# The FFN gate's modulation vector computed by ScalarE and GpSimd during the scans instead of by TensorE within w_in

## The chip, the cores and the metric

The kernel runs on one core of one Trainium2 chip. The metric is the device time of one execution in microseconds (us); lower is better. The core's engines are TensorE (PE in the profile, its weight loads PEld), VectorE (DVE), ScalarE (ACT), GpSimd (POOL) and SyncE (SP), which here only issues DMAs. Each engine works through its own queue in order and waits on semaphores for the others.

## The reference

One layer over 512 latent tokens and 128 context tokens, 640 rows (T) of width 2048 (D). Both groups share the weights; each has its own conditioning vector and so its own modulation:

```python
mod_ctx = (jax.nn.silu(c_ctx) @ w_mod[l] + b_mod[l])
mod_lat = (jax.nn.silu(c) @ w_mod[l] + b_mod[l])
sh1, sc1, g1, sh2, sc2, g2 = jnp.split(mod, 6, axis=-1)      # six vectors of 2048
h = rmsnorm(x, norm1_g) * (1.0 + sc1) + sh1
p = h @ w_in                                                 # 2048 x 5408
o_a, s_fin = rwkv7_bidir(shift(p[..., :3360]), s0)           # scans over the tokens, both ways, 16 heads of 64
o_b = chunk_gmlp(gelu(p[..., 3360:]))
x = x + g1 * (concat([o_a, o_b]) @ w_out)
h = rmsnorm(x, norm2_g) * (1.0 + sc2) + sh2
ff = (silu(h @ w_ffn_gate) * (h @ w_ffn_up)) @ w_ffn_down
x = x + g2 * ff                                              # g2 is used nowhere else
```

The change is about `g2`, the FFN gate: a product of two vectors (latent and context) with the last 2048 of the 12288 columns of `w_mod`, 16.8 MB of float32, plus a bias.

## The kernel before

The stages follow one another in time (us from the start of the profiled execution): the first modulation groups and the norm (to about 120), the w_in projection with everything that prepares the scans (to about 1076), the scans with half of w_out (to about 1382), the rest of w_out with the second norm (to about 1503), and the FFN (to the end).

- **Products in two parts.** Weights arrive as float32 (`raw`). ScalarE rounds them (`hi`, L173), VectorE takes the rest (`lo`, L174), and TensorE multiplies each with the activations in three matmuls of 320 columns. `split` does this for 512 x 128 weights; its tiles come from a pool of three (`st`).
- **w_in.** A loop runs over 160 pieces (40 column blocks of 128, four pieces each; three blocks come earlier). After each piece, `MODR` more steps of the generator `mod_all` are taken. `mod_all` computes four modulation groups one after the other, in the order 2, 4, 3, 5; group 5 is `g2`. Its matmuls (L913, `pm<-wt,cT`) have a weight of two columns (the two conditioning vectors) and 512 moving columns, four of them side by side in the array; then come four transposes (L181) and copies into `modc[g]`.
- **Scans.** Eight head pairs, 13 hops apart, are scanned in 117 hops. A hop advances the active pairs (`recur`): state products on TensorE (`w_ps` L1158, `u_ps` L1178, `s_ps` L1205, `y_ps` L1131 and L1141); `u_ps` is copied into the record `rec` by VectorE (L1182) and ScalarE (L1183), and `s_ps` needs both copies. ScalarE copies the outputs into `Y` (L1146). The records come by DMA (`rec<-d_S`, L1092), eight in flight, each load waiting until an older record has been used. After a pair, `norm` runs on GpSimd (L1240, L1242, L142, L1249, L1252) with squares on ScalarE (L1246) and sums on VectorE (L1247). Every hop also does a share of the w_out products (L1046 to L1048), whose weights go through `split`.
- **Order.** TensorE's order in w_in is the kernel's own by pace rules and by hand; in the scans it is the program's order. The other engines' queues, SP's too, are put in order by a scheduler when the kernel is built: an instruction that is added can move others.
- **w_out, second part.** For each of two halves of the rows and 16 blocks m, `four_blocks` does products (L1489 to L1491), and the tiles `xo1_j`, `xo2_j` (pool `xep`) are first written in its second half.

Of the kernel before, what the change touches and what calls it, by code (L numbers as in the profile page):

```python
# [10 lines left out]
F32 = mybir.dt.float32  # L11
F32R = mybir.dt.float32r
BF16 = mybir.dt.bfloat16
AF = mybir.ActivationFunctionType
ALU = mybir.AluOpType
# [4 lines left out]
P = 128  # L20
D = 2048
KB = D // P
T = 640
NT = T // P
HALF = T // 2
# [21 lines left out]
WAIT = 20  # L47
NW = 8
SUBST = 4.6
MODR = 1.36  # L50
NREC = 8
CHK = (3, 3, 4, 4, 4, 4)
POOLK = (3,)
# [36 lines left out]
def flow_step(ctx: ExitStack, tc, x_prompt, x_sample, state_rwkv, c, c_ctx, w_mod, b_mod,  # L90
# [3 lines left out]
    nc = tc.nc  # L94
    V, S, G, TE = nc.vector, nc.scalar, nc.gpsimd, nc.tensor
# [13 lines left out]
    def tpool(**a):  # L109
        if a.get("space") != DRAM:  # L110
            a["reuse_waits"] = "tile"
        return tc.tile_pool(**a)
# [35 lines left out]
    modc = {g: cp.tile([P, KB, 2], F32, name=f"modc{g}") for g in (2, 3, 4, 5)}  # L148
    cT = cb.tile([P, 2 * KB + 32], F32, name="cT")
# [63 lines left out]
    with ExitStack() as ph:  # L213
# [133 lines left out]
        for j in range(4):  # L347
# [5 lines left out]
            for kb in range(4 * j, 4 * j + 4):  # L353
                hf = p0b.tile([P, T], F32, name="hf")
# [547 lines left out]
        return quad  # L902

    def mod_all():
        for g in (2, 4, 3, 5):
            pm = cur["psum"].tile([P, 512], F32, tag="pmod", name=f"pm{g}")
            quad = load_mod(g, 0)
            for _ in range(4):
                yield
            for kb in range(0, KB, 2):  # L910
                for u in range(2):
                    for j in range(4):
                        TE.matmul(pm[32 * j:32 * j + 2, :], cT[:, 2 * (kb + u):2 * (kb + u) + 2], quad[:, u, j, :],  # L913
                                  start=(kb + u == 0), stop=(kb + u == KB - 1), tile_position=(0, 32 * j))
                for _ in range(2):
                    yield
                if kb + 2 < KB:
                    quad = load_mod(g, kb + 2)
                    for _ in range(4):
                        yield  # L920
            ms = cur["pool"].tile([P, 2, 4, 512], F32, tag=cur["raw"], name=f"ms{g}", bufs=1)[:, 0, 0, :]
            G.memset(ms, 0.0)
            for j in range(4):
                for v in range(2):
                    nc.sync.dma_start(ms[32 * j + v:32 * j + v + 1, :],
                                      b_mod[:, g * D + 512 * j:g * D + 512 * j + 512])
            yield
            yield
            for j in range(4):
                V.tensor_add(ms[32 * j:32 * j + 2, :], pm[32 * j:32 * j + 2, :], ms[32 * j:32 * j + 2, :])  # L930
            mod_cols(cur["tp"], ms, modc[g], tag=cur["tag"])
            yield
# [6 lines left out]
    g = 0  # L939
# [81 lines left out]
    xep = xex.enter_context(tpool(name="xep", bufs=1, side="right"))  # L1021
    obp = [obx.enter_context(tpool(name=n, bufs=1, side="right")) for n in ("oba", "obb")]
    pbig = obx.enter_context(tpool(name="pbig", bufs=2, space=PSUM))
    o_hi, o_lo = {}, {}

    def o_load(kb, src=None):

# [34 lines left out]
    with ExitStack() as ph:  # L1062
# [221 lines left out]
        def wout_b():  # L1284

            for q in range(2):
# [3 lines left out]
                for m in range(KB):  # L1290
# [6 lines left out]
                    for k, c in enumerate(wout(m, q)):  # L1297
                        yield c
                        if q == 0 and k in (0, 2):
# [3 lines left out]
                                TE.transpose(ps[:, t - t0, :], xc[:, t, :], ident)  # L1303
                            S.copy(xc[:, t0:t1, :], ps[:, 0:t1 - t0, :])

        for _ in range(4):
            load_next()
        load_s0(0)
# [15 lines left out]
        with tc.manual_schedule(engines={mybir.EngineType.PE}):  # L1324
            for hop in range(hops):
                if hop == OFF * nxt and nxt < NPAIR:
                    act.append((nxt, recur(nxt)))
                    nxt += 1
                for p, gen in act:
                    next(gen)  # L1330
                for job in list(after):
                    if job[0] < 0:
                        next(job[2], None)
                    elif job[0] in (LATE, LATE + 1):
                        join(job[1], job[0] - LATE)
                for p, gen in list(act):
                    if next(gen, 0) == 0:
                        act.remove((p, gen))
                        after.append([-7, p, norm(p)])
                for job in list(after):  # L1340
                    if job[0] in (LATE + 2, LATE + 3):
                        gate(job[1], job[0] - LATE - 2)
                    job[0] += 1
                    if job[0] > LATE + 3:
                        after.remove(job)
                m3.run(max(0.0, m3.left - REST * 3.2) / (hops - hop))
                if hop == hops - 12:
                    for kb in range(4):
                        o_load(kb)

            assert not act
            (_, p, gen), = after
            for _ in gen:
                pass
            for i, work in enumerate((lambda: join(p, 0), lambda: join(p, 1), lambda: gate(p, 0), lambda: gate(p, 1))):
                while m3.left > (4 - i) * 1.6 - 0.1:
                    m3.run(0.01)
                work()
            m3.drain()
        for kb in range(4, 7):  # L1360
            o_load(kb)
        o_load(7, U[7].bv)
# [74 lines left out]
    with ExitStack() as ph:  # L1437
# [40 lines left out]
        def four_blocks(hf, m, q):  # L1478

            s = slice(HALF * hf, HALF * hf + HALF)  # L1480
            if q == 0:
                pool = pb2 if m % 2 or hf == 0 and m == 4 else pbig
                banks[m] = pool.tile([P, HALF], F32, tag="big", name="big")
            ps = banks[m]
            hi, lo = split(w_out[0, 4 * q * P:(4 * q + 4) * P, m * P:(m + 1) * P], 4,
                           *((wraw, wo) if q or hf or m >= AHEAD else ()))
            for k in range(4):
                kb = 4 * q + k
                TE.matmul(ps, hi[:, k, :], o_hi[kb][:, s], start=(kb == 0), stop=False)  # L1489
                TE.matmul(ps, hi[:, k, :], o_lo[kb][:, s], start=False, stop=False)  # L1490
                TE.matmul(ps, lo[:, k, :], o_hi[kb][:, s], start=False, stop=(kb == 7))  # L1491
            return ps

        for m in range(AHEAD):
            four_blocks(0, m, 0)
        for hf in range(2):
            s = slice(HALF * hf, HALF * hf + HALF)
            for m in range(KB):
                if hf or m >= AHEAD:
                    four_blocks(hf, m, 0)  # L1500
                ps = four_blocks(hf, m, 1)
                if hf and m in (6, 7, 8, KB - 1):
                    for _ in range(2):
                        next(first)
                if sqs and (sqs[0][0] and sqs[0][1] >= 12 or m % 4 == 1):
                    stats()
                add_out(m, [ps, ps], hf)
                nc.sync.dma_start(d_x1[m][:, s], x1T[m][:, s])
                squares(hf, m)
                if hf and m > 1:  # L1510
                    for kb in HALVES[m - 2:m - 1] if m < 14 else HALVES[2 * m - 16:2 * m - 14]:
                        first_half(kb)
                    if 4 <= m < 12:
                        j, i = divmod(m - 4, 2)
                        operand(1 + i, j, x1T[j + 8 * i][:, t1])
# [620 lines left out]
```

## Time and profile before

| what | value |
|---|---|
| median of 3 runs | 3207.54 us (3205.68 to 3216.92) |
| profiled execution | 3204.18 us, span of its instructions 3202.4 us |
| TensorE clock granted, mean | 0.992 |
| TensorE busy | 3084.3 us, 96% of the span |
| VectorE, ScalarE, GpSimd busy | 2341.2, 1461.4, 1220.5 us |
| HBM read | 437.79 MB |

A busy TensorE is not TensorE at its peak, since matmuls overlap: each of the 320-column matmuls is shown with about 310 ns but the next one starts about 147 ns later. A wait row names the engine and line that waited, and what ended the wait; idle time of an engine that nobody waits for costs nothing. Times in the stretches are from the profiled execution's start.

### The profile page before, as it was taken

How to read it: one execution, taken by the hardware profiler on the slowest of the kernel's cores; microseconds unless marked ns; L12 is line 12 of the kernel's file. 1: busy time of each engine (PE TensorE's matmuls, PEld its weight loads, DVE VectorE, ACT ScalarE, POOL GpSimd, SP SyncE). 2: the span in 40 equal slices, each digit the busy share in tenths (PEclk: the TensorE clock that was granted, in tenths of full speed). 3: DMA queues.
4: the chain of work that ended last, by engine and by line, in shares of the span. 5: the costliest groups of instructions: out<-in, count | busy, mean ns of one | idle time of the engine just before them, and what ended most of it. 6: DMA issues, size and time to landing. Idle time of an engine off the chain costs nothing.

```text
span 3202.4 us, 72234 instructions
## 1 busy us (share of the span) xinstructions
PE 3084.3 (96%) x28216; PEld 2859.1 (89%) x28216; DVE 2341.2 (73%) x4107; ACT 1461.4 (46%) x3197; POOL 1220.5 (38%) x1065
## 2 busy tenths in 40 slices
PE   6999999999999999999999999999999999999997
PEld 4788778787878888899999999999999999999997
DVE  4557666676657677767878877777787787878778
ACT  3344544454444444346544444444444444443365
POOL 2001121211122023311366566656665655555542
PEclk9999999999999999999999999999999999999999
DMA  9767786777777688565334433443344364553453
GB/s 371 251 183 202 211 220 174 198 220 191 205 203 212 201 273 256 180 201 158 115 116 127 126 109 119 119 128 121 108 126 127 109 194 152 166 158 120 141 166 122
DMA packets 740438, 550.88 MB, mean 172 GB/s; under 512 B 141056, under 2 KB 673504, under 8 KB 731264
## 3 DMA queue, kind: packets, MB, share of 16 engines
q1 hardware_dynamic: 727136, 532.47, 55.0%
q0 software_dynamic: 10624, 13.23, 1.9%
q8 instruction: 222, 3.64, 0.5%
q14 instruction: 120, 0.98, 0.1%
q10 hardware_dynamic: 2336, 0.57, 0.1%
HBM read 437.79 MB, written 110.95 MB: 171 GB/s over the span
## 4 chain that ended last, share of the span: by engine, by line
PE 44%; DVE 3%; issue 2%; DMA 2%; POOL 1%; ACT 0%; SPq 0%; DVEq 0%; POOLq 0%; ACTq 0%
PE P L1653 15%; PE P L1651 15%; PE P L1650 15%; DVE lo L1431 1%; DMA opd<-d_op 1%; DMA x1d<-d_x 0%; DMA rawd<-in_w_ffn_down_dram 0%; DVE xd L1719 0%; POOL rawd L1559 0%; DVE cd L1909 0%; DVE acc L1890 0%; DVE out L2103 0%; DMA xd<-d_os 0%; ACT hi L1430 0%; PE P L2043 0%
## 5 line engine op out<-in xcount | busy, mean ns | idle before, releaser
L1650 PE MATMUL P<-xo,hi 128*128 128x320 f32 x2352 | 700.0, 309 | 0.2 <-ACT hi L1430 0.2
L1651 PE MATMUL P<-xo,hi 128*128 128x320 f32 x2352 | 700.0, 310 | 0.0
L1431 DVE TENSOR_TENSOR lo<-raw,hi 128x512 fp32r<-128x512 f32 x526 | 521.6, 998 | 158.6 <-ACT hi L1430 156.7
L1430 ACT CAST hi<-raw 128x512 fp32r<-128x512 f32 x526 | 326.7, 622 | 468.4 <-PE P L1651 395.3
L1653 PE MATMUL P<-xo,lo 128*128 128x320 f32 x2352 | 441.7, 310 | 4.6 <-DVE lo L1431 4.6
L1650 PEld LDWEIGHTS P<-xo,hi 128*128 128x128 f32 x2352 | 442.0, 188 | 0.5 <-ACT hi L1430 0.5
L195 PE MATMUL big<-h_hi,hi 128*128 128x320 f32 x1376 | 437.6, 325 | 5.0 <-ACT h_hi L358 2.9
L1651 PEld LDWEIGHTS P<-xo,hi 128*128 128x128 f32 x2352 | 442.2, 188 | 0.0
L196 PE MATMUL big<-h_lo,hi 128*128 128x320 f32 x1376 | 422.8, 314 | 0.7 <-DVE h_lo L359 0.7
L1559 POOL TENSOR_TENSOR raw<-raw 128x512 f32<-128x512 f32 x252 | 409.5, 1634 | 10.1 <-DVE lo L1431 1.8
L1653 PEld LDWEIGHTS P<-xo,lo 128*128 128x128 f32 x2352 | 369.5, 188 | 5.8 <-DVE lo L1431 5.8
L1650 PE MATMUL P<-xd,hi 128*128 128x320 f32 x1232 | 367.9, 310 | 6.1 <-ACT P L2044 2.6
L1651 PE MATMUL P<-xd,hi 128*128 128x320 f32 x1232 | 367.0, 310 | 0.0
L174 DVE TENSOR_TENSOR lo<-raw,hi 128x512 fp32r<-128x512 f32 x268 | 184.5, 693 | 203.0 <-ACT hi L173 200.7
L199 PE MATMUL big<-h_hi,lo 128*128 128x320 f32 x1376 | 323.7, 313 | 0.4 <-DVE lo L174 0.3
L195 PEld LDWEIGHTS big<-h_hi,hi 128*128 128x128 f32 x1376 | 261.5, 190 | 51.4 <-issue 31.1
L1559 POOL TENSOR_TENSOR t<-raw 128x512 f32<-128x512 f32 x84 | 124.4, 1481 | 427.6 <-DMA raw<-in_w_ffn_up_dram 417.6
L173 ACT CAST hi<-raw 128x512 fp32r<-128x512 f32 x268 | 164.5, 617 | 236.4 <-PE big L196 117.6
L1430 ACT CAST hi<-rawd 128x512 fp32r<-128x512 f32 (+1 forms) x288 | 166.9, 586 | 227.0 <-PE P L1651 152.3
L196 PEld LDWEIGHTS big<-h_lo,hi 128*128 128x128 f32 x1376 | 261.2, 190 | 5.9 <-DVE h_lo L359 1.7
L1431 DVE TENSOR_TENSOR lo<-rawd,hi 128x512 fp32r<-128x512 f32 (+1 forms) x288 | 235.9, 826 | 24.7 <-ACT hi L1430 24.5
L1653 PE MATMUL P<-xd,lo 128*128 128x320 f32 x1232 | 236.6, 310 | 4.8 <-DVE lo L1431 4.6
(404 smaller groups left out, 6115.2 us busy)
## 6 DMA issues: line engine op xcount, KB each, us to landing
wt<-in_w_mod_dram SPq DMA_DIRECT2D x96, 1024.0 KB
raw<-in_w_ffn_gate_dram SPq DMA_DIRECT2D x182, 256.0 KB
raw<-in_w_ffn_up_dram SPq DMA_DIRECT2D x182, 256.0 KB
rec<-d_S SPq DMA_DIRECT2D x80, 576.0 KB
raw<-in_w_in_dram SPq DMA_DIRECT2D x172, 256.0 KB
rawd<-in_w_ffn_down_dram SPq DMA_DIRECT2D x128, 256.0 KB
raw<-in_w_out_dram SPq DMA_DIRECT2D x96, 256.0 KB
xd<-d_os SPq DMA_DIRECT2D x66, 320.0 KB
```

What stands on the lines that cost most here:

```text
L173: S.copy(hi, raw)
L174: V.tensor_sub(lo, raw, hi.bitcast(F32))
L195: TE.matmul(halves[hf], hi[:, k, :], h_hi[:, kb, s], start=(kb == 0), stop=False)
L196: TE.matmul(halves[hf], hi[:, k, :], h_lo[:, kb, s], start=False, stop=False)
L199: TE.matmul(halves[hf], lo[:, j - 4 * q, :], h_hi[:, j, s], start=False, stop=(j == KB - 1))
L1430: S.copy(hi[:, 0:nk], raw[:, 0:nk])
L1431: V.tensor_sub(lo[:, 0:nk], raw[:, 0:nk], hi[:, 0:nk].bitcast(F32))
L1559: G.tensor_tensor(out=o[:, 0:nk], in0=p[:, 0:nk], in1=q[:, 0:nk], op=ALU.subtract)
L1650: TE.matmul(ps, hi[:, k, :], xk[:, 0, :], start=q == 0 and k == 0 and not filled, stop=False)
L1651: TE.matmul(ps, hi[:, k, :], xk[:, 1, :], start=False, stop=False)
L1653: TE.matmul(ps, lo[:, k, :], x(i, 4 * q + k)[:, 0, :], start=False, stop=q == nq - 1 and k == nk - 1 and last)
```

## The change

`mod_all` leaves group 5 out, and `MODR` goes from 1.36 to 1.02, so that its three groups still spread over w_in. A new generator `gate_mod` is advanced once or twice in each hop of the scans, 128 steps in all. Per 128 rows of `w_mod` and 1024 of its columns one DMA brings 512 KB (`wm`, two buffers); per 512 columns and conditioning vector ScalarE multiplies the block by the vector's 128 values, one per partition (`wc`, three buffers), and GpSimd adds the product to an accumulator (`am`, eight of them, in the tiles that `xo1_j` and `xo2_j` take later). What is left is a sum over the 128 partitions: 32 matmuls with one column of ones, after block 12 of the first half of w_out (`gate_cols`).

```diff
-MODR = 1.36
+MODR = 1.02
...
-        for g in (2, 4, 3, 5):
+        for g in (2, 4, 3):
...
+        wm = ph.enter_context(tpool(name="wm", bufs=2))
+        def gate_mod():
+            for j in range(4):
+                for v in range(2):
+                    a = xep.tile([P, 512], F32, tag=f"xo{1 + v}_{j}", name="am")
+                    macc[j, v] = a
+                    G.memset(a, 0.0)
+                    nc.sync.dma_start(a[0:1, :], b_mod[:, 5 * D + 512 * j:5 * D + 512 * j + 512])
+            for kb in range(KB):
+                for u in range(2):
+                    w = wm.tile([P, 2, 512], F32, tag="wm", name="wm")
+                    nc.sync.dma_start(w.rearrange("p j n -> p (j n)"),
+                                      w_mod[0, kb * P:kb * P + P, 5 * D + 1024 * u:5 * D + 1024 * u + 1024])
+                    for j in range(2):
+                        for v in range(2):
+                            a = macc[2 * u + j, v]
+                            wc = wm.tile([P, 512], F32, tag="wc", name="wc", bufs=3)
+                            S.activation(wc, w[:, j, :], AF.Copy, scale=cT[:, 2 * kb + v:2 * kb + v + 1])
+                            G.tensor_tensor(out=a, in0=a, in1=wc, op=ALU.add)
+                            yield
+        gmod = gate_mod()
...
                 m3.run(max(0.0, m3.left - REST * 3.2) / (hops - hop))
+                for _ in range(2 if hop % 4 == 3 else 1):
+                    next(gmod, None)
...
+        for _ in gmod:
+            pass
...
+        def gate_cols():
+            ps = pb2.tile([P, HALF], F32, tag="big", name="pgm")
+            for kb in range(KB):
+                for v in range(2):
+                    TE.matmul(ps[:, 2 * kb + v:2 * kb + v + 1], macc[kb // 4, v][:, P * (kb % 4):P * (kb % 4) + P],
+                              ones[:, 0:1], start=True, stop=True)
+            V.tensor_copy(modc[5].rearrange("p k v -> p (k v)"), ps[:, 0:2 * KB])
...
+                if not hf and m == 12:
+                    gate_cols()
```

Line numbers of the scan stage and behind it are higher by 25 or more in the changed kernel; ScalarE's products are its L1325, GpSimd's sums L1326.

How the queues stand, at three places.

ScalarE, at the norm of the first pair (`sq` are its squares, L1183 the copies that the scan's next product waits for). Before:

```order
L1246 ACTIVATE sq<-Y 128x320 [waits DVE_49,Pool_49]
L1246 ACTIVATE sq<-Y 128x320 [waits Pool_49]
L1183 COPY rec<-u_ps 64x2x64 [waits DMAHW4_49,DVE_49]
L1304 COPY x1T<-pxT 128x128 [waits PE_49]
L1183 COPY rec<-u_ps 64x2x64 [waits DMAHW6_49,DVE_49]
L1183 COPY rec<-u_ps 64x2x64 [waits DMAHW0_49,DVE_49]
```

The same place in the changed kernel:

```order
L1246 ACTIVATE sq<-Y 128x320 [waits Pool_49]
L173 CAST hi<-raw 128x512 [waits DMAHW5_49]
L1233 CAST gate<-graw 128x128 [waits DMAHW7_49]
...
L1325 ACTIVATE wc<-wm,cT 128x512 [waits DMAHW4_49]
L1325 ACTIVATE wc<-wm,cT 128x512
L1183 COPY rec<-u_ps 64x2x64 [waits DVE_49]
L1304 COPY x1T<-pxT 128x128 [waits PE_49]
L1325 ACTIVATE wc<-wm,cT 128x512
L1325 ACTIVATE wc<-wm,cT 128x512 [waits Pool_49]
L1183 COPY rec<-u_ps 64x2x64 [waits DVE_49]
```

Four products now stand among the copies; the fourth waits for GpSimd, since it needs the first one's buffer.

GpSimd, from the end of the norm of the first pair to the beginning of the second's, in the changed kernel (before, the same rows stand without the one of L1326):

```order
L1249 TENSOR_SCALAR ys<-ys 128x10 [waits DVE_49]
L142 TENSOR_TENSOR ys<-ys,mhalf 128x10 [waits Pool_49]
L1252 TENSOR_TENSOR Y<-Y,ys 128x320 [waits Activation_49,Pool_49]
L1252 TENSOR_TENSOR Y<-Y,ys 128x320 [waits Activation_49]
L1326 TENSOR_TENSOR am<-am,wc 128x512 [waits Activation_49] x16
L1240 TENSOR_SCALAR ys<-ys 128x10 [waits Activation_49]
L1242 TENSOR_TENSOR Y<-Y,ys 128x320 [waits Pool_49]
```

The sums stand in groups between the norms: 32 ahead of the first pair's, then 16, 4 within the second, 16, 3 within the third, 13, 20, 12, 4 within the sixth and 8.

SP, at the begin of the scans (`raw<-in_w_out_dram` are w_out's weights, `rec<-d_S` the records). Before:

```order
L1097 DMA s_13703<-in_state_rwkv_dram 128x2x64 [waits DMAHW7_49,DMAHW0_49,PE_49]
L172 DMA raw<-in_w_out_dram 128x4x128 [waits Activation_49]
L172 DMA raw<-in_w_out_dram 128x4x128 [waits DMAHW1_49,Activation_49]
...
L1227 DMA bv<-d_bv 128x640 [waits DMAHW5_49]
L1092 DMA rec<-d_S 128x2x576 [waits DMAHW6_49,PE_49,Activation_49]
```

In the changed kernel:

```order
L1319 DMA wm<-in_w_mod_dram 128x1024
...
L1315 DMA am<-in_b_mod_dram 1x512 [waits DMAHW1_49,Pool_49]
L1092 DMA rec<-d_S 128x2x576 [waits DMAHW2_49,PE_49,Activation_49]
L1092 DMA rec<-d_S 128x2x576 [waits DMAHW3_49,PE_49,Activation_49]
L172 DMA raw<-in_w_out_dram 128x4x128 [waits DMAHW4_49]
L1319 DMA wm<-in_w_mod_dram 128x1024 [waits DMAHW5_49]
```

The first loads of w_out's weights in the scans now stand behind two record loads that wait for TensorE's first outputs.

More of the change, by code (lines that the diff above doesn't have):

```diff
@@ L1023, in flow_step @@
     pbig = obx.enter_context(tpool(name="pbig", bufs=2, space=PSUM))
-    o_hi, o_lo = {}, {}
+    o_hi, o_lo, macc = {}, {}, {}
     def o_load(kb, src=None):
```

## Prediction

> **What bounds the kernel now.** I read the page's busy times and slices first, then the chain that ended last, then windows around the places that the change touches.
>
> ```profile
> PE 3084.3 (96%) x28216; PEld 2859.1 (89%) x28216; DVE 2341.2 (73%) x4107; ACT 1461.4 (46%) x3197; POOL 1220.5 (38%) x1065
> ...
> PE   6999999999999999999999999999999999999997
> ...
> POOL 2001121211122023311366566656665655555542
> ...
> PE 44%; DVE 3%; issue 2%; DMA 2%; POOL 1%; ACT 0%; SPq 0%; DVEq 0%; POOLq 0%; ACTq 0%
> ```
>
> TensorE is busy in nearly every slice, and the chain that ended last lies on it. GpSimd looks free in slices 14 to 17, where the scans are. The windows (busy time of PE, PEld, DVE, ACT, POOL; then clock, DMA share, GB/s) say how free:
>
> ```profile
> 800.00:1030.00 230.00, 222.25 (x2682) 190.48 (x2681) 155.93 (x317) 109.30 (x233) 46.72 (x75) 0.99 0.76 212
> ...
> 1097.00:1322.00 225.00, 217.90 (x3861) 184.70 (x3863) 169.76 (x562) 93.98 (x448) 64.82 (x84) 1.00 0.83 263
> ...
> 0.00:80.00 80.00, 54.75 (x360) 32.45 (x361) 35.96 (x85) 28.35 (x40) 17.79 (x35) 0.96 1.02 371
> ```
>
> TensorE fills 97% both in w_in's last quarter (first row) and in the scans' hops 0 to about 102, over which the 128 new steps are spread (second row). So what TensorE no longer does in w_in is gained almost in full, and whatever holds it up in the scans is lost almost in full. GpSimd has 225 - 65 = 160 us free there.
>
> **What is removed.** Group 5 of the modulation, the last of four: 64 matmuls (128 records), four transposes, and 16.8 MB of loads.
>
> ```profile
> 800.00:1030.00 230.00, 17.58 (x128) 2.48 (x128) 0.99 0.76 212
> ...
> 1017.51 0.45 PE L199 MATMUL big<-h_hi,lo 128*128 128x320 f32 x2
> 1017.90 1.90 PE L913 MATMUL pm<-wt,cT 128*2 128x512 f32 x16
> 1019.73 0.42 PE L195 MATMUL big<-h_hi,hi 128*128 128x320 f32 x1
> ...
> L181 PE MATMUL ptm<-ident,ms x16: 272/273/302, 325.0 to 1039.9; 128*128 128x128 f32 x16
> ```
>
> The first row is L913 alone in that window: 17.6 us of busy time. The timeline gives the true cost: two L199 records start 0.147 us apart, so L195 would have begun at 1017.51 + 2 x 0.147 = 1017.80; it began at 1019.73, 1.93 us later for 16 records, or 15.4 us for 128. Smaller bursts cost more each, the transposes at most 4 x 0.27 = 1.1 us. I take 18 us, between 15 and 20. VectorE's four bias sums, GpSimd's memset and SP's loads leave with it, off the path; the three groups that stay are only spread wider.
>
> **What TensorE gets back.** 32 matmuls with 128 x 128 float32 weights and one column, in w_out, where it has no gap. No row shows that shape. The nearest are float32 matmuls with 128 columns and with 64 x 64 weights:
>
> ```profile
> 1004.53 1.05 PE L776 MATMUL psp<-wspT,vt 128*128 128x128 f32 x8
> ...
> 1101.39 0.45 PE L1158 MATMUL w_ps<-ST,rec 64*64 64x64 f32 x8
> ```
>
> A float32 matmul makes two records, so there are 64. At 1.05/8 = 0.131 us that is 8.4 us, at 0.45/8 = 0.056 us 3.6 us. The weights are L776's, the moving part is nearly nothing: 6 us. The copy of 32 columns on VectorE hides beside w_out's matmuls.
>
> **What GpSimd gets.** 128 sums of 128 x 512, and eight memsets.
>
> ```profile
> L1242 POOL TENSOR_TENSOR Y<-Y,ys x32: 718/723/1230, 1149.5 to 1357.1; 128x320 f32<-128x320 f32 x32
> ...
> L1559 POOL TENSOR_TENSOR raw<-raw x252: 1285/1634/1837, 1550.8 to 2588.7; 128x512 f32<-128x512 f32 x126
> ...
> L922 POOL MEMSET ms<- x4: 522/526/547, 303.1 to 1024.5; 128x512 f32 x4
> ...
> 1149.12 0.27 POOL L1240 TENSOR_SCALAR ys<-ys 128x10 f32<-128x10 f32 x1 [60.44 <-ACT Y L1146]
> ...
> 1152.83 0.21 POOL L1249 TENSOR_SCALAR ys<-ys 128x10 f32<-128x10 f32 x1
> ...
> 1159.13 1.40 POOL L1252 TENSOR_TENSOR Y<-Y,ys 128x320 f32<-128x320 f32 x2
> 1181.81 0.26 POOL L1240 TENSOR_SCALAR ys<-ys 128x10 f32<-128x10 f32 x1 [21.27 <-ACT Y L1146]
> ...
> 1212.30 0.40 POOL L1240 TENSOR_SCALAR ys<-ys 128x10 f32<-128x10 f32 x1 [19.04 <-ACT Y L1146]
> ```
>
> L1559 is the same shape: 1.285 us undisturbed, 1.634 median in the FFN. In the scans L1242 runs mostly at its minimum (718, 723), so I take 1.35 us. Together 128 x 1.35 + 8 x 0.53 = 177 us for 160 us of free time: 17 us too much even if all were level.
>
> It isn't level. A norm holds GpSimd from 1149.1 to 1160.5, and 7.7 us of that lie behind the last squares (1152.8, L1249). In the changed order ScalarE comes right after those squares to four products; three have buffers, the fourth waits until GpSimd has finished the norm and one sum: 1160.5 + 1.35 = 1161.9. Behind it in ScalarE's queue stands L1183:
>
> ```profile
> 1152.35 0.90 ACT L1246 ACTIVATE sq<-Y 128x320 f32<-128x320 f32 x2 [0.28 <-DVE ys L1247]
> ...
> 1155.20 0.26 ACT L1183 COPY rec<-u_ps 64x128 f32<-64x128 f32 x1 [1.38 <-DVE rec L1182]
> ...
> 1156.48 0.64 PE L1205 MATMUL s_ps<-rec 128*64 128x64 f32 x16
> ...
> L173 ACT CAST hi<-raw 128x512 fp32r<-128x512 f32 x33 | 20.4, 618 | 41.7 <-PE big L1047 33.3 <-DMA raw<-in_w_out_dram 7.7 <-ACT gss L1316 0.7
> ```
>
> A product costs about what the cast L173 does, 0.62 us. So the copy slips from 1155.2 to 1161.9 + 0.6 = 1162.5, 7.3 us, and TensorE's `s_ps` from 1156.5 to about 1162.8, 6.3 us: all later scan products are behind it in TensorE's queue, w_out's too. I walked the other pairs by the same rule: each product waits for the third sum before it, sums run at 1.35 us, norms in their places. The second norm, with four sums inside and 16 behind it that ScalarE meets within nine hops, costs 16 us; the fourth, 8; the others 1 to 5 each, in all 38. TensorE's lead over ScalarE at those places (1.3 us above) takes away about 8. I take 30 us, between 10 (the level case less what the three buffers and pauses take up) and 46 (no lead at all).
>
> **The begin of the scans.** w_out's weights are now loaded behind two record loads that wait for TensorE's first outputs.
>
> ```profile
> 1096.21 1.11 SPq L172 DMA_DIRECT2D raw<-in_w_out_dram  x2
> ...
> 1101.43 0.62 ACT L173 CAST hi<-raw 128x512 fp32r<-128x512 f32 x1 [7.43 <-DMA raw<-in_w_out_dram]
> ...
> 1108.96 0.88 SPq L1092 DMA_DIRECT2D rec<-d_S  x2
> ...
> 1110.30 0.42 PE L1046 MATMUL big<-oh,hi 128*128 128x320 f32 x1
> ```
>
> Issue was at 1096.2 and the cast could start at 1101.4, 5.2 us later. Issued at 1108.96 + 0.88, the cast ends at 1109.8 + 5.2 + 0.6 = 1115.7; TensorE wants the block at 1110.3. That is 5 us, between 0 and 8. The further loads: 32 of 512 KB make 16.8 MB in 225 us, 75 GB/s on top of 263; the first 80 us moved 371, so I price bandwidth at nothing. If it doesn't reach, records come late and each microsecond counts. SP issues 40 more DMAs of about 0.55 us, 22 us in 225, at nothing. A `wm` load waits there for ScalarE to be done with an older one, with record loads behind it; eight records in flight cover that unless ScalarE is late by more than their lead, and then it is late already. ScalarE's 128 x 0.62 = 79 us on 94 leave it at 77% and cost only through order, as above.
>
> **The sum**, on the profiled execution: 3204.2 - 18 + 6 + 30 + 5 = 3227.2. The median of the runs lies 3207.54 - 3204.18 = 3.4 us above that execution: 3230.6, so 3230.
>
> **Rivals.**
> - *VectorE becomes the scans' limit.* GpSimd's work slows some of VectorE's:
>
> ```profile
> L1167 DVE TENSOR_TENSOR W<-w_ps,rec x144: 281/289/297, 1103.7 to 1347.8; 64x128 f32<-64x128 f32 x144
> ...
> L1189 DVE TENSOR_TENSOR SG<-SN,gend x64: 271/278/826, 1107.6 to 1346.6; 128x128 f32<-128x128 f32 x64
> ...
> L1431 DVE TENSOR_TENSOR lo<-raw,hi 128x512 fp32r<-128x512 f32 x526 | 521.6, 998 | 158.6 <-ACT hi L1430 156.7
> ...
> L174 DVE TENSOR_TENSOR lo<-raw,hi 128x512 fp32r<-128x512 f32 x268 | 184.5, 693 | 203.0 <-ACT hi L173 200.7
> ```
>
> W, with one operand from PSUM, never changes; SG goes to 826 ns; `lo` takes 693 ns up to w_out and 998 in the FFN, where GpSimd is at work. At 0.3 us for 72 SG and 33 `lo` that is 32 us more on a VectorE at 170 of 225; half of it on the path gives 3245. [...] Against it as the likeliest: while ScalarE waits, VectorE idles.
> - *GpSimd's load counts only on average.* If pauses even out the bursts, the scans grow by 17 us, not 30, and the begin by 0: 3207.5 - 18 + 6 + 17 = 3212.
> - *The lag is absorbed, no loss.* ScalarE's products could run far enough ahead of the copies that GpSimd is waited for at no place that TensorE needs. It decides if a sum costs under (160 - 4)/128 = 1.2 us and the norm's tail is met with free buffers; L1559's minimum of 1.285 us and the order at the first norm speak against it. Then 3207.5 - 18 + 6 + 2 = 3197, not slower.
> - *More than the matmuls is gained.* w_in's DMA share of 0.76 falls and waits for weights go too; with 25 us gained and nothing lost in the scans it would be under 3191.
>
> **Chances.** Forecast 0.50; VectorE 0.15; average 0.20; absorbed 0.12; more gained 0.03. Half a per cent, 16 us, is about what a measurement here can tell from no change: 3191.5 to 3223.5. The forecast's own range, 3222 to 3240, is all but 0.02 slower: slower 0.63, same 0.34 (0.20 + 0.12 + 0.02), faster 0.03. The range 3205 to 3260: at the bottom -20, +4, +10, +0 give 3201, at the top -15, +8, +46, +8 with some of VectorE's 16 give about 3260; outside lie most of the absorbed and the faster cases and a tail above.
>
> **What the profile after would show.** w_in: L913 with 384 records, the first `w_ps` some 18 us earlier. Scans: GpSimd over 85% busy with L1326 near 1.35 us; ScalarE's L1325 idle behind `am` L1326; `s_ps` waiting for L1183 right after the first, second and fourth norm, some 6, 13 and 6 us; the stretch from the first `w_ps` to the last `pO` longer by about 35 us. At the begin, TensorE waits some 5 us for a `hi` of w_out. w_out: L1528 within 4 to 8 us. The forecast is wrong if L1326 takes under 1.2 us, if ScalarE's wait falls where TensorE has work that doesn't need it, or if TensorE makes the time up in the hops without sums.

## The result: slower by 2.5%, where 0.7% was forecast

The changed kernel takes 3291.6 us (3287.8 to 3298.9, 4 runs) against 3208.2 us before (3205.7 to 3216.9, 4 runs). The ratio is 1.0254, 95% interval 1.0236 to 1.0271: 83 us more, where the prediction said 23 and its range ended at 52. The direction was right, the size wrong by a factor of almost four.

### The profile page after: what moved, and what is told of

It reads as the page before. It is cut to its first block, busy times and chain, and to the rows that moved or that the text cites. A ratio compares the mean times of both kernels' runs of the same rounds, so it can differ in the third digit from the quotient of the medians.

```text
span 3297.1 us, 72382 instructions
## 1 busy us (share of the span) xinstructions
PE 3114.9 (94%) x28148; PEld 2896.1 (88%) x28148; DVE 2358.3 (72%) x4102; ACT 1547.2 (47%) x3325; POOL 1393.5 (42%) x1200
## 4 chain that ended last, share of the span: by engine, by line
PE 72%; DVE 9%; DMA 7%; POOL 5%; issue 4%; ACT 2%; SPq 0%; DVEq 0%; POOLq 0%; ACTq 0%
PE P L1693 15%; PE P L1690 15%; PE P L1691 15%; PE big L195 4%; PE big L196 4%; PE big L199 4%; POOL am L1326 2%; PE pm L913 1%; DMA raw<-in_w_in_dram 1%; PE big L1518 1%; PE pG L658 1%; PE big L1519 1%; PE big L1520 1%; DVE lo L1460 1%; PE pblk L850 1%
## 5 line engine op out<-in xcount | busy, mean ns | idle before, releaser
L1599 POOL TENSOR_TENSOR raw<-raw 128x512 f32<-128x512 f32 x252 | 411.4, 1642 | 10.1 <-DVE lo L1460 1.8
L173 ACT CAST hi<-raw 128x512 fp32r<-128x512 f32 x268 | 164.7, 617 | 222.0 <-PE big L196 101.2
L1460 DVE TENSOR_TENSOR lo<-rawd,hi 128x512 fp32r<-128x512 f32 (+1 forms) x288 | 229.0, 802 | 27.4 <-ACT hi L1459 27.0
```

The lines of the kernel that those rows point to most:

```text
L173: S.copy(hi, raw)
L1460: V.tensor_sub(lo[:, 0:nk], raw[:, 0:nk], hi[:, 0:nk].bitcast(F32))
L1599: G.tensor_tensor(out=o[:, 0:nk], in0=p[:, 0:nk], in1=q[:, 0:nk], op=ALU.subtract)
```

## The profile after

The page's lines that answer to those of before: busy times, the slices of TensorE, GpSimd and the granted clock, and the chain that ended last.

```profile
PE 3114.9 (94%) x28148; PEld 2896.1 (88%) x28148; DVE 2358.3 (72%) x4102; ACT 1547.2 (47%) x3325; POOL 1393.5 (42%) x1200
...
PE   6999999989999877899999999999999999999997
...
POOL 2002221212121577731155665665665655555542
PEclk9999999999999888999999999999999999999999
...
PE 72%; DVE 9%; DMA 7%; POOL 5%; issue 4%; ACT 2%; SPq 0%; DVEq 0%; POOLq 0%; ACTq 0%
```

TensorE has 68 records fewer and is busy 30.6 us longer. The PEclk row says why: in slices 13 to 15 (counted from 0), the scans, the granted clock is in its eighties, in per cent of full speed. The stages follow in windows, of the kernel before (three rows) and after (three rows): up to the first `w_ps`, from there to the last `pO`, and the rest but for the last 11 to 16 us. Behind the busy times of PE, PEld, DVE, ACT and POOL stand clock, DMA share and GB/s.

```profile
0.00:1101.40 1101.40, 1033.94 (x11604) 859.14 (x11604) 707.06 (x1436) 497.81 (x1034) 180.00 (x297) 0.98 0.74 217
1101.40:1375.70 274.30, 264.66 (x4514) 226.19 (x4513) 201.39 (x644) 109.19 (x506) 87.32 (x112) 1.00 0.72 227
1375.70:3186.00 1810.30, 1785.06 (x12103) 1773.45 (x12098) 1421.78 (x2016) 851.23 (x1643) 952.33 (x655) 1.00 0.45 135
```

```profile
0.00:1101.80 1101.80, 1024.20 (x11472) 863.47 (x11472) 704.87 (x1430) 499.85 (x1036) 183.86 (x305) 0.97 0.70 202
1101.80:1455.30 353.50, 290.65 (x4514) 245.22 (x4513) 228.43 (x644) 192.44 (x633) 254.04 (x240) 0.89 0.70 224
1455.30:3286.00 1830.70, 1800.09 (x12170) 1787.44 (x12166) 1418.26 (x2023) 854.86 (x1657) 955.61 (x656) 0.99 0.44 134
```

The profiled execution is the longest of its four (3298.9 us; that of the kernel before, 3204.2 us, is shorter than its four timed runs), so the spans differ by 94.7 us and not by 83. Of these, nothing is gained up to the scans (+0.4), the scans take 79.2 more, and the part behind them 15 more. In the scans TensorE has the same 4514 records. Its idle time rose from 9.6 to 62.9 us (stretch less busy time), and its busy time, with the same work, by 26.0 us, because matmuls ran at a lower clock: 75.1 us of the stretch are at half the clock (0.50), TensorE is busy in 52.1 of them, and by my estimate the same matmuls would take about half of that at the full clock, 26 us less (one-column records start 0.112 us apart at the full clock and 0.213 at half, experiment 10). What TensorE waited for in the scans (us in total, times, longest):

```profile
PE big L1046 <- ACT hi L173: 27.0, 4, 8.1
PE s_ps L1205 <- ACT rec L1183: 14.1, 11, 4.9
PE w_ps L1158 <- DVE SN L1213: 5.6, 7, 2.2
```

The largest wait is not the one that the prediction walked through (`s_ps`), but w_out's product waiting for its weights. One of the four, on the queues of SyncE, ScalarE and TensorE:

```profile
1144.34 12.15 SPq L1092 DMA_DIRECT2D rec<-d_S  x6
...
1162.00 0.46 SPq L172 DMA_DIRECT2D raw<-in_w_out_dram  x1
...
1168.60 0.62 ACT L173 CAST hi<-raw 128x512 fp32r<-128x512 f32 x1 [2.43 <-DMA raw<-in_w_out_dram]
...
1169.27 0.64 PE L1046 MATMUL big<-oh,hi 128*128 128x320 f32 x1 [7.52 <-ACT hi L173]
```

Six record loads, each waiting for an older record to be used, hold SyncE for 12 us. The load of the weights stands behind them, is issued at 1162.0, and TensorE stands still until 1169.3. In the same queue the new loads wait too, for ScalarE to be done with an older block, and hold what stands behind them:

```profile
SPq L1319 <- ACT wc L1325: 23.2, 7, 7.0
```

## Experiments

"Stretch" below is the time from the first `w_ps` to the last `pO` in a kernel's profile. Ratios are against the kernel before on the same chip. One row of windows for each kernel gives the stretch and the busy times in it. Each kernel has one profile, and profiles of the same scans differ: 274.2, 276.7 and 274.7 us in the kernel before and experiments 1 and 2, 353.5 and 347.1 us in the changed kernel and experiment 10. An edit can also move instructions that it doesn't name, since the scheduler orders the queues anew. ScalarE's last product starts at 1400.6 us in the changed kernel, at 1356.5 with the loads on ScalarE's queue (experiment 4), at 1315.3 without sums too (5), and at 1231.5 without most loads (`e14_products_only`).

**1. Nothing added, group 5 left out.** The kernel `e1_left_out` drops the generator and the one-column matmuls from the changed kernel:

```diff
-                for _ in range(2 if hop % 4 == 3 else 1):
-                    next(gmod, None)
...
-            ps = pb2.tile([P, HALF], F32, tag="big", name="pgm")
...
+            V.memset(modc[5], 0.0)
```

> The changed kernel without what it adds: no loads, products, sums and one-column matmuls; the gate vector is set to zero, so its share of the output is missing. Group 5 stays out of w_in. This prices the first term of the sum alone. As the prediction has it, 18 us are gained: 3190 us (3187 to 3193), first w_ps near 1083 us. Rival (the removed matmuls stood where TensorE would else wait, and the waits bring the half clock with them): nothing is gained in w_in, first w_ps at 1098 to 1103 us, the rest as before: 3203 to 3210 us.

Measured: 3200.6 us against 3207.8, ratio 0.9975 (0.9963 to 0.9986): 7 us gained, not 18 and not nothing. The stretch up to the first `w_ps`:

```profile
0.00:1095.50 1095.50, 1020.17 (x11470) 860.00 (x11470) 704.01 (x1432) 498.99 (x1037) 178.84 (x296) 0.97 0.71 203
```

The L913 and L181 matmuls that left were 18.7 us of busy time, but TensorE is busy only 13.8 us less (1033.9 to 1020.2), so the others ran 4.9 us longer, at a clock of 0.97; and it is idle 7.8 us more (67.5 to 75.3). 18.7 - 4.9 - 7.8 = 6.0, and `w_ps` starts 5.9 us earlier. So a good part of the removed matmuls stood where TensorE else waits. All the profiles here agree in this: up to the first `w_ps`, the three kernels with group 5 in w_in have 34 to 41 us at half the clock and TensorE idle for 67 to 68 us, the twelve without it 51 to 89 and 70 to 79 us. The start of `w_ps` itself is less sure, 1100.2 to 1102.0 us in the three and 1093.4 to 1106.9 in the twelve, so the gain is better read from the whole times: 7 us, between 4 and 12.

**2. The same with `MODR` back at 1.36** (`e2_left_out_early`), so that the three groups stand between the same pieces as before:

```diff
-MODR = 1.02
+MODR = 1.36
```

> As the kernel that only leaves group 5 out (the gate vector zero), but with MODR back at 1.36: the three groups that stay are done after three quarters of w_in and stand between the same pieces as before, the last quarter has none. If the loss of the 18 us comes from spreading three groups wider (other pieces left without a filler), this gains 10 to 18 us: 3190 to 3198 us. If the last quarter needs the filler as much, it is 3200 to 3210 us, and the trace shows half-clock stretches between 800 and 1100 us.

Measured: 3201.5 us, ratio 0.9977 (0.9965 to 0.9989). The same 6 to 7 us, the second case: it isn't the spreading. In its profile 15.0 us are at half the clock between 800 us and the first `w_ps`, against 6.8 in the kernel before.

**3. No sums** (`e4_no_sums`): the changed kernel without GpSimd's L1326.

```diff
-                            G.tensor_tensor(out=a, in0=a, in1=wc, op=ALU.add)
```

> The changed kernel without GpSimd's 128 sums (the products of ScalarE and all loads stay; the gate vector is only the bias). ScalarE has no GpSimd to wait for, and VectorE no GpSimd beside it. If the buffers behind GpSimd's sums are the cause (the prediction's term) or VectorE blocked by GpSimd, the scan stretch falls from 353 us back to 275 to 290 us, with no half clock in it: 3215 to 3235 us. If the cause is SyncE's queue, where w_out's weights stand behind record loads, the four waits of w_out's products for hi (27 us) and a half clock behind each stay: stretch 305 to 330 us, 3250 to 3275 us.

**4. w_mod's loads on ScalarE's queue** (`e5_wm_act`), everything else kept:

```diff
-                    nc.sync.dma_start(w.rearrange("p j n -> p (j n)"),
+                    nc.scalar.dma_start(w.rearrange("p j n -> p (j n)"),
```

> The changed kernel with the 32 loads of w_mod issued from ScalarE's queue instead of SyncE's; the order at building then puts w_out's loads ahead of the record loads again, as before the change. Products and sums stay. If SyncE's queue is the main cause, the waits of w_out's products for hi fall from 27 us to under 5 and the half clock behind them goes: stretch 300 to 320 us, 3245 to 3265 us. If GpSimd (through the buffers or beside VectorE) is the main cause, the stretch stays at 335 us or more: 3275 to 3295 us.

Measured: 3267.5 us (ratio 1.0187, 1.0168 to 1.0205) without sums, 3276.5 us (1.0212, 1.0197 to 1.0227) with the loads moved. Their stretches, in this order:

```profile
1098.60:1422.70 324.10, 275.63 (x4513) 231.85 (x4513) 203.80 (x644) 189.55 (x633) 90.84 (x112) 0.95 0.77 244
...
1100.80:1437.30 336.50, 293.93 (x4514) 248.31 (x4513) 232.29 (x643) 188.74 (x630) 254.78 (x240) 0.91 0.73 233
```

Without sums the waits for `hi` stay, as in the second case of experiment 3:

```profile
PE big L1046 <- ACT hi L173: 28.7, 5, 8.9
```

They are SyncE's. With the loads moved they are gone, but only 17 us of the 79 with them, which is the second case of experiment 4. Both causes are real and neither is the whole.

**5. Both cures at once** (`e6_no_sums_wm_act`): the edits of 3 and 4 together.

> Both cures at once: w_mod's loads on ScalarE's queue and no sums on GpSimd (the gate vector is only the bias). ScalarE's 128 products and all loads stay. If SyncE's queue and GpSimd's sums are the whole cause, the scan stretch is 277 to 290 us, with at most two half-clock windows: 3218 to 3232 us (what is left is the one-column matmuls' 15 us and some of ScalarE's). If ScalarE's products themselves or the bandwidth of the loads cost too, it is over 300 us and over 3240 us.

**6. Sums replaced by fills** (`e7_memsets`): GpSimd is nearly as busy and frees ScalarE's buffers about as late, but reads nothing.

```diff
-                            G.tensor_tensor(out=a, in0=a, in1=wc, op=ALU.add)
+                            for n in (512, 512, 256):
+                                G.memset(wc[:, 0:n], 0.0)
```

> As the kernel with w_mod's loads on ScalarE's queue (3276 us, scan stretch 336.5 us, VectorE busy 232 us in it), but each sum is replaced by fills of the same product buffer with zeros, 1280 columns in place of one sum of 512, about the same time on GpSimd (1.3 us). GpSimd writes and reads nothing; ScalarE waits for the buffers as before. The gate vector is only the bias. If VectorE blocked by GpSimd's reads is what is left, its busy time falls back to about 202 us, and the stretch to 295 to 315 us: 3235 to 3255 us. If GpSimd's lateness (the prediction's term) is what is left, nothing changes: stretch 328 to 345 us, 3268 to 3285 us.

Measured: 3244.7 us (1.0111, 1.0096 to 1.0126) and 3268.0 us (1.0182, 1.0165 to 1.0199). The stretches, and what ScalarE waits for in the first of the two:

```profile
1095.60:1398.00 302.40, 274.18 (x4513) 232.26 (x4513) 204.22 (x643) 183.93 (x625) 87.59 (x114) 0.98 0.78 258
...
1093.40:1417.30 323.90, 284.39 (x4513) 240.78 (x4513) 202.66 (x644) 185.37 (x626) 240.00 (x482) 0.93 0.76 243
...
ACT wc L1325 <- DMA wm<-in_w_mod_dram: 27.3, 15, 4.7
```

With fills VectorE's busy time is back from 232.3 to 202.7 us. One of its instructions, SG, with sums (experiment 4; median 428 ns) and with fills (281 ns):

```profile
L1189 DVE TENSOR_TENSOR SG<-SN,gend x64: 272/428/1390, 1105.6 to 1408.3; 128x128 f32<-128x128 f32 x64
L1189 DVE TENSOR_TENSOR SG<-SN,gend x64: 272/281/812, 1102.3 to 1388.4; 128x128 f32<-128x128 f32 x64
```

The stretch is 12.6 us shorter than with sums. That is the most that the slower VectorE costs there, since GpSimd is also 14.8 us less busy with fills (240.0 against 254.8); the stretch lies between the two cases that were expected. GpSimd's time alone costs 323.9 - 302.4 = 21.5 us, and TensorE's waits for ScalarE's copies grow with it (without sums, then with fills):

```profile
PE s_ps L1205 <- ACT rec L1183: 13.8, 15, 3.3
PE s_ps L1205 <- ACT rec L1183: 23.0, 18, 4.7
```

And even with neither sums nor SyncE's queue, 28 us were left, the second case of experiment 5.

**7. Loads alone** (`e10_loads_only`), **products alone** (`e14_products_only`), **a third buffer** (`e15_three_wm`). All have the loads on ScalarE's queue and no sums. The first has no products; the second loads two blocks once and multiplies them 128 times; the third is the kernel of experiment 5 with three buffers for the blocks, and one instead of three for the products, which no sum reads. The main lines of the three edits, each against that kernel:

```diff
-                            S.activation(wc, w[:, j, :], AF.Copy, scale=cT[:, 2 * kb + v:2 * kb + v + 1])
```

```diff
-                    w = wm.tile([P, 2, 512], F32, tag="wm", name="wm")
+                    if kb:
+                        w = ws[u]
+                    else:
+                        w = ws[u] = wm.tile([P, 2, 512], F32, tag=f"wm{u}", name="wm", bufs=1)
```

```diff
-        wm = ph.enter_context(tpool(name="wm", bufs=2))
+        wm = ph.enter_context(tpool(name="wm", bufs=3))
...
-                            wc = wm.tile([P, 512], F32, tag="wc", name="wc", bufs=3)
+                            wc = wm.tile([P, 512], F32, tag="wc", name="wc", bufs=1)
```

> The kernel with w_mod's loads on ScalarE's queue, without products and sums: the loads go nowhere, and the gate vector is only the bias. With ScalarE's products and no sums the scan stretch was 302 us, against 274 before the change. If ScalarE's products standing ahead of the record copies are what is left, the stretch is 274 to 280 us, the granted clock there 0.99 or more, and the time 3215 to 3228 us. If the loads (their bandwidth, or ScalarE issuing them) cost too, the stretch is 285 us or more: 3230 us or more.

> ScalarE's 128 products without the loads: two blocks of w_mod are loaded once, and all products read them; no sums (the gate vector is only the bias). With loads on ScalarE's queue and products the scan stretch was 302 us, with these loads alone 308, before the change 274. If ScalarE waiting in order for the loads (to land, or to be issued) is what is left, the stretch is 274 to 284 us with the clock at 0.99 or more: 3213 to 3226 us. If the products' own 92 us on ScalarE's queue hold the record copies up, it is 292 us or more: 3232 us or more.

> The kernel with w_mod's loads on ScalarE's queue, products and no sums (stretch 302 us, ScalarE 27 us waiting for blocks of w_mod to land), with three buffers for the blocks instead of two. If the wait for the landing is what is left, ScalarE's wait falls under 10 us and the stretch to 280 to 292 us: 3220 to 3234 us. If it is the products, or the bandwidth, nothing changes: stretch 298 to 306 us, 3240 to 3250 us.

Measured: 3243.6 us (1.0109, 1.0094 to 1.0124), 3229.4 us (1.0059, 1.0041 to 1.0077), 3232.6 us (1.0066, 1.0045 to 1.0087). The stretches in this order, one wait of ScalarE in the first kernel, and what is left of its wait for blocks in the third:

```profile
1094.00:1402.10 308.10, 282.53 (x4513) 240.71 (x4513) 202.33 (x644) 109.04 (x506) 88.56 (x114) 0.92 0.78 252
...
1098.80:1385.30 286.50, 269.75 (x4513) 229.09 (x4513) 202.61 (x643) 180.33 (x620) 87.97 (x112) 0.99 0.71 219
...
1099.80:1387.00 287.20, 268.80 (x4511) 228.88 (x4512) 203.81 (x644) 185.86 (x626) 88.99 (x114) 0.99 0.82 271
...
ACT Y L1146 <- DMA wm<-in_w_mod_dram: 11.8, 3, 5.2
...
ACT wc L1325 <- DMA wm<-in_w_mod_dram: 0.5, 1, 0.5
```

The first of these is the second case by its numbers, but it didn't separate what I meant it to: with nobody reading the blocks, the next load into a buffer waits on ScalarE's queue for the last one to land, and holds what stands behind it (11.8 us at `Y`, in three waits). The other two do. The products alone cost 12.3 us (286.5 against 274.2), between my two theories; TensorE's waits for ScalarE's copies are 6.5 us there and 1.2 in the kernel before. These products stand in the first half of the scans, so the 12.3 us are a price for that place. With three buffers all loads are there, at 271 GB/s, and the stretch is 287.2, the first case: so it isn't bandwidth, but ScalarE waiting in order for a block to land, 15 us.

**8. GpSimd without ScalarE** (`e12_no_products`): GpSimd adds the loaded blocks themselves and issues their loads.

```diff
-                    nc.sync.dma_start(w.rearrange("p j n -> p (j n)"),
+                    nc.gpsimd.dma_start(w.rearrange("p j n -> p (j n)"),
...
-                            S.activation(wc, w[:, j, :], AF.Copy, scale=cT[:, 2 * kb + v:2 * kb + v + 1])
-                            G.tensor_tensor(out=a, in0=a, in1=wc, op=ALU.add)
+                            G.tensor_tensor(out=a, in0=a, in1=w[:, j, :], op=ALU.add)
```

> The changed kernel without ScalarE's products: GpSimd adds the loaded blocks themselves (a wrong gate vector) and issues their loads itself, so neither ScalarE nor SyncE waits for GpSimd or for these loads. GpSimd's 128 sums stay, with VectorE beside them. If GpSimd holds TensorE up through ScalarE, as the prediction has it, what is left is VectorE blocked by GpSimd's reads: stretch 280 to 295 us, 3220 to 3242 us. If GpSimd's own lateness in the norms is the limit, the stretch stays over 310 us: over 3250 us.

Measured: 3322.3 us, ratio 1.0353 (1.0332 to 1.0374), the worst of all: the second case, and more than it said. Waits of TensorE, ScalarE and VectorE in the stretch:

```profile
PE u_ps L1178 <- DVE W L1167: 61.5, 12, 24.7
...
ACT sq L1246 <- POOL Y L1242: 67.8, 21, 26.6
...
DVE ys L1247 <- ACT sq L1246: 55.9, 16, 24.9
```

GpSimd comes late to a norm, behind a row of sums; ScalarE's squares wait for it, VectorE's sums of squares wait for those in order, and behind these stands W, without which TensorE has no `u_ps`. So GpSimd's lateness has a second way to TensorE, through VectorE. Its size here is this kernel's own: GpSimd also issues 30 loads in the stretch and waits 19.2 us for blocks to land, which it doesn't do in the changed kernel. There the same wait of VectorE is 12.0 us in all, where before the change it was 5.1.

**9. What a pause of TensorE costs.** In the kernel before, at four hops, TensorE waits for 13 fills of GpSimd (`e8_idle`), or does 50 needless matmuls (`e9_busy`):

```diff
+                if hop in (30, 43, 56, 69):
+                    TE.matmul(pz[:, 0, 0:64], ident, zz[:, 0:64], start=True, stop=True)
+                    for _ in range(13):
+                        G.memset(zz, 0.0)
+                    TE.matmul(pz[:, 0, 0:64], ident, zz[:, 0:64], start=True, stop=True)
```

```diff
+                if hop in (30, 43, 56, 69):
+                    for _ in range(50):
+                        TE.matmul(pz.rearrange("p a b -> p (a b)")[:, 0:HALF], o_hi[8][:, 0:P], o_hi[8][:, 0:HALF],
+                                  start=True, stop=True)
```

> The kernel before with four pauses of TensorE in the scans (hops 30, 43, 56, 69), each by a small product that waits for 13 fills on GpSimd, about 7 us; nothing else is added or left out. If a pause costs its own length, the time is that of the kernel with four equally long rows of matmuls: 3208 + 28 = 3236 us. If the half clock follows a pause (one or two stretches of 3.4 us each), it is 7 to 20 us more: 3243 to 3256 us, and the granted clock in the scans is below 1.00.

> The kernel before with four rows of 50 needless matmuls of 320 columns at the same four hops, 50 x 0.147 = 7.3 us each; the results go nowhere. Other engines have as long a break as in the kernel with four pauses, TensorE has none. By both theories the granted clock in the scans stays 1.00 and the time is 3208 + 29 = 3237 us (3228 to 3240, if VectorE uses the breaks to catch up).

Measured: 3251.0 us (1.0126, 1.0111 to 1.0141) with pauses, 3239.6 us (1.0090, 1.0075 to 1.0105) with matmuls. The stretches, with pauses and with matmuls, the wait itself, and three windows around the first pause:

```profile
1102.00:1417.60 315.60, 275.63 (x4530) 235.46 (x4529) 201.53 (x644) 108.02 (x504) 114.54 (x164) 0.94 0.64 198
...
1100.20:1403.50 303.30, 294.60 (x4714) 255.53 (x4713) 200.87 (x644) 108.23 (x505) 87.36 (x112) 1.00 0.67 206
...
PE pz L1354 <- POOL zz L1353: 32.0, 4, 9.0
...
1150.00:1162.70 12.70, 10.65 (x183) 8.75 (x175) 9.66 (x33) 6.14 (x27) 10.65 (x15) 1.00 1.00 305
1162.70:1172.90 10.20, 4.30 (x49) 3.50 (x51) 2.48 (x7) 1.98 (x4) 5.27 (x11) 0.50 0.61 186
1172.90:1203.60 30.70, 27.80 (x510) 23.78 (x508) 21.54 (x72) 12.46 (x61) 12.30 (x18) 1.00 0.72 221
```

The matmuls cost what they last (29.1 us for 4 x 50 x 0.147 = 29.4) at a clock of 1.00. The pauses are 32.0 us of waiting, and the stretch grows by 41.3: TensorE is busy 11.0 us more, of which the eight small products with their halves are 4.3 and the rest, 6.7 us, slower matmuls. The second case came true. The second window shows it: 10.2 us at half the clock, which begin during the pause (1161.0 to 1168.6) and last 4.3 us past it.

**10. The one-column matmuls spread** (`e11_cols_spread`): one step of two matmuls behind each block of w_out from the fourth on.

```diff
             for kb in range(KB):
+                yield
                 for v in range(2):
...
-                if not hf and m == 12:
-                    gate_cols()
+                for _ in range(1 if hf or m > 2 else 0):
+                    next(cols, None)
```

> The changed kernel with the 32 one-column matmuls spread: two behind each block of w_out from the fourth one on, instead of all behind one block. The work is the same. If the half clock of 10.2 us behind the matmuls comes from 10 us in a row of them, it goes: the part behind the scans falls from 1841.9 us to 1834 to 1838 us, and the time by 4 to 8 us, to 3284 to 3288 us. If only the matmuls themselves cost, the part stays at 1840 to 1844 us and the time at 3288 to 3294 us.

Measured: 3289.3 us, ratio 1.0256 (1.0226 to 1.0287), within the uncertainty of the changed kernel's; by the time it is the second case, by the part behind the scans the first. In its profile the part behind the scans (3291.5 - 1454.0) is 1837.5 us; the nine profiles with the matmuls in a row have 1840.5 to 1845.1 there, and five without them 1825.0 to 1833.3. In the changed kernel, the ten us of these matmuls and what follows:

```profile
L1528 PE MATMUL pgm<-ones,am x64: 164/255/352, 1512.7 to 1522.7; 128*128 128x1 f32 x64
...
1516.30:1526.50 10.20, 10.20 (x46) 10.20 (x46) 0.80 (x2) 0.22 (x1) 0.00 (x0) 0.50 0.10 27
```

This row of one-column matmuls keeps TensorE busy in the profile (10.20 of 10.20 us in the window), and yet the half clock comes (0.50): the first 33 records start 0.112 us apart, the others 0.213. Spread, no half clock comes there and the records of a group stay 0.112 us apart. The part is 3 to 8 us shorter than with the row, but profiles without any of these matmuls differ by as much, and the whole time doesn't show it: that spreading gains time is not shown.

## Why the prediction was wrong, point by point

Three steps of the sum failed most: w_in's -18 was -7, the +5 for SyncE's queue was 17, and ScalarE's products and loads, put at nothing, were 28. Measured, w_in's -7, the scans' 79 and 12 behind them make 84, against 83 by the runs. The stretch of the scans, added up from the kernels above (each step a difference of two profiles, split into TensorE's idle time and its busy time, in which the half clock shows):

| step | stretch, us | cost, us | idle, us | busy, us |
|---|---|---|---|---|
| before | 274.2 | | | |
| ScalarE's 128 products alone (`e14_products_only`) | 286.5 | 12.3 | 7.1 | 5.1 |
| and their loads, with ScalarE waiting for them to land (`e6_no_sums_wm_act`) | 302.4 | 15.9 | 11.5 | 4.4 |
| and GpSimd's time (`e7_memsets`) | 323.9 | 21.5 | 11.3 | 10.2 |
| and GpSimd's sums beside VectorE in place of fills, with 14.8 us more of GpSimd (`e5_wm_act`) | 336.5 | 12.6 | 3.1 | 9.5 |
| and the loads on SyncE's queue (changed kernel) | 353.5 | 17.0 | 20.3 | -3.3 |

The ratios of the whole times give 17, 23, 10 and 13 us for the last four steps, each to some 7 us, which agrees. The prices hold for this order of steps: moving the loads to SyncE's queue costs 21.7 us without sums (324.1 against 302.4), 17.0 with them.

- **w_in, -18.** Failed: "what TensorE no longer does in w_in is gained almost in full". The size of the removed work was right (18.7 us of records), the reading of 97% busy was not: 11 to 12 us of it had filled waits or kept the clock up. Alone it gains 7 us.
- **One-column matmuls, +6, between 3.6 and 8.4.** The matmul was priced rightly: at 0.112 us a record 64 take 7.2 us. What failed is the clock, which fell within the row: it took 10.1 us. The part behind the scans is 15 us longer in the changed kernel's profile than in that of the kernel before, and on average 12 us longer in the nine profiles with the row than in the five without. A clock that falls was no part of the bounds.
- **Scans, +30.** The mechanism stood, as one of five. GpSimd's sums took what was said (1.281 us median, 1.319 mean, against 1.35), but GpSimd wasn't saturated: busy 254.0 of 353.5 us, in a stretch that other waits had made longer too. Its time costs 21.5 us, through ScalarE's buffers and, as experiment 8 showed, through the norm and VectorE; how these two share it isn't settled. The places were wrong: no `s_ps` waits at the first norm, and the longest wait, 4.9 us, came late at 1391.6. At the first norm ScalarE stood waiting for w_out's weights (1168.6), and its products came behind that. The order shown ahead of the prediction has this cast (L173) between the squares and the products; the walk passed over it.
- **Begin of the scans, +5, between 0 and 8.** The first wait was as said, 4.3 us at 1115.6. Failed: the term was priced at one place. The same stands at three more (7.5, 8.1 and 7.1 us), since loads that wait for records to be used stand ahead of w_out's at each of them, and `wm` loads that wait for ScalarE (23.2 us in all) stand in the same queue; the runs don't separate the two. The order of the queue could be read ahead of the run to its end; I read its begin.
- **ScalarE's products and loads, at nothing.** Failed: "cost only through order" was true of the mechanism and no reason for a zero. 12.3 us for 128 products of 0.72 us ahead of record copies, 15.9 us with the loads, of which 15.2 go with a third buffer, that is with the wait for a block to land. Both were measured with the loads on ScalarE's queue or left out; in the changed kernel ScalarE's own waits for blocks to land are 16.0 us. SyncE's loads were priced through issue time and bandwidth, not through the engine that waits for them in order.
- **VectorE, a rival at 0.15.** It came true beside the rest: in the scans the median of SG went from 278 to 522 ns, VectorE was busy 228.4 us against 201.4, and up to 12.6 us of it lay on the path. With fills, which read nothing, in place of sums, VectorE's 232.3 us fall to 202.7 and the median of SG from 428 to 281 ns (experiment 6).
- **The clock, in no step.** 26 of the 79 us in the scans are matmuls at half clock, spread over the rows of the table. No term of the sum had it.

The rivals were set against each other, but each engine's lateness adds to the others' in a stage where TensorE had 9.6 us of idle time in 274. No kernel here with the gate vector computed beat the kernel before: leaving it out gains 7 us, and summing it over the partitions in a row of matmuls takes TensorE 10.1 us.

## What to carry to other kernels

Work moved off a full TensorE isn't gained if it filled waits (here 18.7 us of records gave 7 us); leave it out in one run and see what the stage gives before building its replacement. Work moved onto "free" engines cost through their queues here (79 us in the scans): for each added instruction ask what it waits for (a buffer, a landing, a record) and what stands behind it, at every place and not only the first. Short waits of TensorE cost more than their length here where the clock fell behind them: 32.0 us of pauses made the stretch 41.3 us longer (experiment 9).

## What the runs showed of the hardware

In the changed kernel's trace the stretches at half clock in the scans last 3.41, 6.83, 10.24 or 13.65 us, one to four times 3.41. Six windows of about that length, of the kernel with w_mod's loads on ScalarE's queue, the first busy time being TensorE's:

```profile
1182.70:1186.10 3.40, 3.40 (x81) 3.08 (x80) 3.14 (x8) 2.90 (x11) 3.40 (x4) 1.00 1.04 371
1186.10:1189.50 3.40, 1.56 (x18) 1.22 (x16) 1.57 (x1) 2.27 (x8) 3.40 (x4) 1.00 1.13 340
1189.50:1192.90 3.40, 3.01 (x29) 2.78 (x30) 2.16 (x7) 0.26 (x1) 1.26 (x1) 0.51 1.03 377
1192.90:1196.40 3.50, 2.86 (x16) 2.01 (x16) 1.38 (x3) 2.79 (x9) 2.07 (x2) 0.50 0.67 182
1196.40:1199.80 3.40, 3.40 (x31) 2.95 (x33) 2.45 (x4) 2.54 (x6) 3.40 (x4) 0.50 0.67 258
1199.80:1203.20 3.40, 3.40 (x67) 2.81 (x67) 2.50 (x6) 1.27 (x6) 3.23 (x5) 1.00 0.70 191
```

TensorE is busy 1.56 of 3.40 us in the second window, 46%, and the third has half the clock (0.51). Here it stayed up to the fifth window, the first full one at half clock (3.40 of 3.40 us), and the sixth is fast again (1.00). No pause of TensorE in this kernel's scans is longer than 3.1 us, and yet 61 of the 336 us are at half clock. In the profiles of all fifteen kernels here, cut into such windows from 120 to 1500 us, 140 of 143 at full clock that were busy for less than half were followed by one at half clock, 22 of 60 between 50 and 60%, and 24 of 5465 above that (seven of these 24 at a row of one-column matmuls). None of the 125 windows at half clock that were busy under 80% was followed by a fast one.
